# A five-branch decoder layer on one Trainium2 core: gate projections of three branches made earlier and kept in DRAM, and units between the steps of a triangular inverse

## The chip, the cores and the metric

One Trainium2 chip, one of its cores. The metric is the device time of one execution of the whole kernel in microseconds (us), lower is better. Three executions of the kernel before took 3696.6 to 3701.26 us, median 3699.76 us.

## What is computed

One decoder layer over 2048 tokens of width 1024. A normalised input h is projected once by a wide matrix; the columns are shared out among five branches (`mem`, `ret`, `rwkv`, `ssd`, `gla`) and five gates of 1024 columns each. Every branch makes an output o_m of 512 (mem: 256) columns; the gated sum of their up-projections goes through an output matrix. Cut to what matters here:

```
h = rms_norm(x, norm_g)
p = h @ w_in                      # branch inputs, and gates: 5 x 1024 columns
o_m = branch_m(p_m)               # rwkv: a recurrence over time, o_ret, o_gla, o_ssd, o_mem likewise
g = sigmoid(gates).reshape(b, t, 5, d)
merged = sum over m of  g[:, :, m] * (o_m @ w_up_m)
x = x + merged @ w_out
return rms_norm(x, final_norm_g)
```

## The kernel before, in words

Time is cut into four super-chunks of 512 tokens; `run` works through them one after the other, and in each through the branches mem, ret, rwkv, ssd, gla. Data lies as [128 rows of a feature, 512 tokens]. A float32 matrix product is made of three fp32r products of high and low parts (`mm3`), so a **projection** of 128 output columns is 24 matmuls of 128x512 (`proj`, 8 row tiles by 3) and an **up-projection** of 128 columns is 12 (4 row tiles by 3). Weights are split into high and low parts in the first super-chunk (ScalarE `L378`, GpSimd `L379`), stored in DRAM, and from then on loaded from there (`load_w`, two tiles of 512 KB for a projection, one for an up-projection; four buffers `wt`).

For each branch eight gate projections (`gate`: a projection, then ScalarE's tanh into an `s` tile) and eight up-projections (`up`: product, VectorE's scalar_tensor_tensor with the tanh, addition to `merged`) are packed as **units** in a queue `self.fq`, a gate and an up in turn (`inter`). The next branch's code calls `self.fill(n)` at places where its own chain would leave TensorE without work; each call takes n units from the queue. The numbers are in the table `K.FILL`. A scheduler then orders each engine's instructions; the engines run their lists in order. The units' products go to the PSUM tag `acc`, three buffers in turn.

`rwkv` is the branch with the longest chain: `rwkv_prep`, then `rwkv_sys`, which inverts 32 triangular 64x64 matrices at once, then `rwkv_chain` with eight steps. In `rwkv_sys` VectorE runs the **inverse pass**, a serial chain of 31 pairs of multiply and reduce of growing size (`L1195` the reduce) and two transposes (`L1198`, `L1200`); `fill(FILL["sys"][0])` stands behind it, so its units run on TensorE beside it. After the pass, `lower` and `corner` are each four times two sets of eight 32x32 matmuls, with copies by VectorE (`L1215`) and ScalarE between them: the **corner stage**.

At the end of a super-chunk comes the **tail**: the second half of gla finishes (`finish`: a sum by matmul with `ones_r`, a chain of ten VectorE operations, a cast on ScalarE, a subtraction on GpSimd, for each of two heads). In the kernel before the eight gate projections of gla stand there, then eight up-projections of gla, between which the next super-chunk's normalised input `xhi`, `xlo` is made (`xhat_units`; one buffer, so all readers of the old one must be done), then the projections of the next super-chunk. SyncE's queue (SP) issues nearly all DMAs, in order.

```
            us = self.gate_units("gla", o, self.nc.vector if last else None)
            for gate, _ in us:
                gate()
            ...
            for k in range(KT):
                if not last:
                    xu[k]()
                us[k][1]()
```

Of the kernel before, what the change touches and what calls it, by code (L numbers as in the profile page):

```python
# [9 lines left out]
F32 = mybir.dt.float32  # L10
F32R = mybir.dt.float32r
I32 = mybir.dt.int32
AF = mybir.ActivationFunctionType
# [4 lines left out]
P = 128  # L18
T = 512
SEQ = 2048  # L20
D = 1024
KT = D // P
# [53 lines left out]
BR = {"ret": 0, "gla": 1, "ssd": 2, "rwkv": 3, "mem": 4}  # L76
# [68 lines left out]
class K:  # L145
# [131 lines left out]
    def nm(self, s):  # L277
# [2 lines left out]

    NS = 42

    FILL = {"mem": (2, 0, 2, 2, 1, 1, 3, 3), "ret": (1, 3, 0), "late": (0, 0, 0, 0), "sys": (12, 3), "chain":
            (2, 3, 2, 1, 1, 2, 4, 3), "norm": 0, "ssd": (6, 0, 3, 4, 4), "gla": (3, 1, 2, 3, 1), "eng": (0, 1,
            0, 1, 0, 1, 0, 0, 1, 1, 1, 1, 1), "rope": (3, 3)}

# [79 lines left out]
    def pick(self, i):  # L366
        return (self.nc.gpsimd, self.nc.vector)[K.FILL["eng"][i]]

# [184 lines left out]
    def mem(self, sc):  # L553
# [33 lines left out]
        def turn(p, c2, h, e):  # L587
            tp = self.ps("br")
            for j in range(4):
                self.tr(tp[:, j * P:(j + 1) * P], e[:, j * P:(j + 1) * P])  # L590
            t4 = tp.rearrange("p (i m t) -> p i m t", i=2, m=2)
            for m in range(2):
                o4 = pT[p][2 * h + m][:, c2 * 256:(c2 + 1) * 256].rearrange("p (i t) -> p i t", i=2)
                nc.any.tensor_copy(out=o4, in_=t4[:, :, m, :])
# [28 lines left out]
        for i, b in enumerate(blocks):  # L623
            nxt = probs(*blocks[i + 1]) if i < 7 else None
            self.fill(K.FILL["mem"][i])
            turn(*b, e)
            if i == min(K.FILL["rope"][sc > 0], 6):
                self.tables = self.rope_tables(sc)
# [103 lines left out]
    def ret(self, sc):  # L732
# [6 lines left out]
        for p in range(2):  # L739
# [32 lines left out]
            ys = [self.ps("y") for _ in range(2)]  # L772
            self.fill(K.FILL["ret"][0])
            for j in range(2):
                for c in range(4):
                    cs_ = slice(c * P, (c + 1) * P)
                    self.mm(ys[j][:, cs_], V[c][:, (2 * p + j) * P:(2 * p + j + 1) * P], pts[j][:, cs_],
                            start=(c == 0), stop=False)
            self.fill(K.FILL["ret"][1])
            for c in range(4):  # L780
                cs_ = slice(c * P, (c + 1) * P)
                for j in range(2):
                    r = slice(64 * j, 64 * j + 64)
                    self.mm(ys[j][:, cs_], S[c][r, :], qh[r, cs_], start=False, stop=(c == 3))
            res += self.finish_pair(sc, "ret", p, ys, self.cv["one"], K.FILL["ret"][2])
        return res
# [371 lines left out]
    def rwkv_sys(self, AR, KB):  # L1158

        nc = self.nc  # L1160
# [3 lines left out]
        for i in range(4):  # L1164
# [12 lines left out]
            for g in range(4):  # L1177
                r, b = slice(32 * g, 32 * g + 32), g % 2
# [23 lines left out]
        for i in range(4):  # L1202
            for g in range(4):
                r, b = slice(32 * g, 32 * g + 32), g % 2
                (nc.scalar.copy, nc.gpsimd.tensor_copy)[g % 2](
                    Ab[i][r, :, 32 * b:32 * b + 32], xa[r, :, i * 8:i * 8 + 8].rearrange("s c j -> s j c"))
        def lower(i, after=None):
            zp = self.ps("br")
            zs = self.s((P, 8, 32), tag="zs", bufs=2)
            for q in range(2):  # L1210
                r1 = slice(64 * q, 64 * q + 32)
                r2 = slice(64 * q + 32, 64 * q + 64)
                for j in range(8):
                    self.mm(zp[r2, j * 32:j * 32 + 32], Ab[i][r1, j, 32:64], T11[r1, :, i * 8 + j], after=after)
                nc.vector.tensor_copy(zs[r2], zp[r2, 0:256].rearrange("p (j t) -> p j t", t=32))  # L1215
            return zp, zs

        def corner(i, zp, zs):
            for q in range(2):
                r1 = slice(64 * q, 64 * q + 32)  # L1220
                r2 = slice(64 * q + 32, 64 * q + 64)
                for j in range(8):
                    self.mm(zp[r1, 256 + j * 32:256 + j * 32 + 32], zs[r2, j, :], Ab[i][r2, j, 32:64])
                nc.scalar.copy(Ab[i][r1, :, 32:64], zp[r1, 256:512].rearrange("p (j t) -> p j t", t=32))
# [2 lines left out]
        z = lower(0, self.last)  # L1227
        for i in range(4):
            nxt = lower(i + 1) if i < 3 else None
            corner(i, *z)  # L1230
            z = nxt
        return Ab
# [116 lines left out]
        return self.rwkv_fin(sc, BV, sg)  # L1349


    def gate_units(self, key, o, eng=None):
        nc = self.nc
        nk = BRK[key]
        first = self.merged is None
        if first:
            self.merged = [None] * KT
        merged = self.merged
        us = []
        for d in range(KT):  # L1360
            th = []

            def gate(d=d, th=th):
                g = self.proj(f"gate{8 * BR[key] + d}")
                t = self.s()
                self.act(t, g, AF.Tanh, scale=0.5)
                th.append(t)

            def up(d=d, th=th):
                w = self.load_w(("wu_" + key, d), nk)  # L1370
                ps = self.ps("acc")
                self.mm3(ps, w, lambda k: o[k], nk)
                t = th[0]
                if first:
                    m = self.xp.tile([P, T], F32, tag=f"mg{d}", name=self.nm("mg"))
                    merged[d] = m
                    self.stt(m, t, 1.0, ps, ALU.add, ALU.mult)
                else:
                    self.stt(t, t, 1.0, ps, ALU.add, ALU.mult)
                    (eng or self.pick({"ret": 0, "rwkv": 1, "ssd": 2, "gla": 3}[key])).tensor_tensor(  # L1380
                        merged[d], merged[d], t, ALU.add)

            us.append((gate, up))
        return us

    @staticmethod
    def inter(us):

        g, u = [a for a, _ in us], [b for _, b in us]
        out = g[:2]  # L1390
        for i in range(len(us)):
            out.append(u[i])
            out += g[i + 2:i + 3]
        return out
# [130 lines left out]
    def run(self):  # L1525
        for sc in range(self.nsc):
            last = sc + 1 == self.nsc
            self.merged = None
            o = self.mem(sc)
            self.fill(99)  # L1530
            for key, nxt in (("mem", "ret"), ("ret", "rwkv"), ("rwkv", "ssd"), ("ssd", "gla")):
                us = self.gate_units(key, o)
                self.fq += self.inter(us)
                if nxt == "ssd" and not last:
                    rs, self.bg = self.xhat_stats(self.xsrc(sc + 1), T)
                o = getattr(self, nxt)(sc)
                if nxt != "ret":
                    self.fill(99)
            for u in self.bg:
                u()  # L1540
            self.bg = []
            us = self.gate_units("gla", o, self.nc.vector if last else None)
            for gate, _ in us:
                gate()
            if not last:
                self.xh, xu = self.xhat_units(sc + 1, rs[0])
            hl = []
            for k in range(KT):
                if not last:
                    xu[k]()  # L1550
                us[k][1]()
            for k in range(KT):
                hl.append(self.half_split(self.merged[k]))
            self.fq = self.out_units(sc, hl, last)
        self.fill(99)
# [82 lines left out]
```

## Time and profile before

| | |
|---|---|
| median of three executions | 3699.76 us |
| profiled execution | 3696.7 us, of which the span from first to last instruction 3694.9 us |
| TensorE (PE) busy | 3513.3 us, 95% of the span, 20304 matmuls |
| VectorE (DVE) busy | 1978.8 us, 54% |
| ScalarE (ACT), GpSimd (POOL) busy | 984.3 us, 900.1 us |
| mean granted TensorE clock | 0.959 of full |
| DMA | 639.57 MB, mean 173 GB/s |

Busy matmuls are pipelined and their ends are modelled; "idle before" in brackets is the time in which the engine had nothing running, and what ended it. The granted clock (PEclk) is 1.00 at the 2.4 GHz level and 0.50 at the 1.2 GHz level.

### The profile page before, as it was taken

The page shows a single profiled execution, that of the slowest core. Times are in us where ns is not written, and L with a number is a line of the kernel's source. Part 1 is how long each engine was busy: PE and PEld are TensorE (multiplying, and loading weights), DVE is VectorE, ACT ScalarE, POOL GpSimd, SP SyncE. Part 2 cuts the span into 40 slices and gives each one's busy share as a digit, 9 for nine tenths or more (in the row PEclk, how much of TensorE's full clock was granted, in tenths as well). Part 3 has the DMA queues.
Part 4 walks back from the last instruction along what each step waited for, and adds up shares of the span by engine and source line. Part 5 has one row for each costly group of instructions (what it writes and reads, how often), then busy time and mean ns, then how long its engine had stood idle before and what let it go on. Part 6 is the DMA issues. An engine that isn't in the chain of part 4 may idle for free.

```text
span 3694.9 us, 51559 instructions
## 1 busy us (share of the span) xinstructions
PE 3513.3 (95%) x20304; PEld 2805.7 (76%) x20304; DVE 1978.8 (54%) x3189; ACT 984.3 (27%) x1796; POOL 900.1 (24%) x919
## 2 busy tenths in 40 slices
PE   7988898999999999999999999999999998999998
PEld 5766777777777777888877777778887867778887
DVE  6377457635444865653353783663345376464243
ACT  4233224342422311312131322322122132131212
POOL 3556325455311410211101321021100132020110
PEclk9989789999999989999999998999999998999999
DMA  6655435676764533545565552345465554344555
GB/s 216 229 177 199 153 121 203 213 256 220 273 210 153 159 120 112 183 157 168 175 214 176 162 169 91 131 149 187 154 220 181 170 158 130 106 148 151 169 169 193
DMA packets 226530, 639.57 MB, mean 173 GB/s; under 512 B 25184, under 2 KB 46192, under 8 KB 226288
## 3 DMA queue, kind: packets, MB, share of 16 engines
q1 hardware_dynamic: 225856, 635.76, 51.7%
q8 instruction: 160, 2.62, 0.3%
q14 instruction: 82, 0.67, 0.1%
q10 hardware_dynamic: 432, 0.52, 0.0%
HBM read 486.76 MB, written 145.23 MB: 171 GB/s over the span
## 4 chain that ended last, share of the span: by engine, by line
PE 55%; DVE 15%; ACT 2%; issue 1%; DMA 1%; SPq 0%; POOL 0%; DVEq 0%; ACTq 0%
PE acc L305 42%; PE br L305 7%; DVE s L302 7%; PE y L305 4%; DVE s L299 3%; DVE blk L299 2%; DVE blk L1195 1%; PE br L317 1%; ACT s L296 1%; DMA s<-in_xT_dram 1%; DVE s L329 0%; ACT blk L1179 0%; DMA wt<-kw 0%; DVE s L339 0%; DVE s L322 0%
## 5 line engine op out<-in xcount | busy, mean ns | idle before, releaser
L305 PE MATMUL acc<-xhi,wt 128*128 128x512 f32 x5632 | 1834.6, 400 | 46.3 <-DVE s L299 15.8
L305 PEld LDWEIGHTS acc<-xhi,wt 128*128 128x128 f32 x5632 | 1076.2, 192 | 299.1 <-ACT s L296 24.9
L305 PE MATMUL acc<-xlo,wt 128*128 128x512 f32 x2816 | 1126.7, 400 | 2.2 <-DVE xlo L1516 1.5
L305 PEld LDWEIGHTS acc<-xlo,wt 128*128 128x128 f32 x2816 | 539.5, 192 | 117.1 <-issue 4.3
L305 PE MATMUL acc<-s,wt 128*128 128x512 f32 (+1 forms) x2448 | 599.0, 395 | 15.4 <-DVE s L302 7.4
L305 PEld LDWEIGHTS acc<-s,wt 128*128 128x128 f32 x2448 | 454.1, 190 | 115.3 <-ACT wt L378 14.1
L302 DVE SCALAR_TENSOR_TENSOR s<-s,acc 128x512 f32<-128x512 f32 x192 | 131.2, 684 | 632.0 <-PE acc L305 344.5
L379 POOL TENSOR_TENSOR wt<-wr,wt 128x512 fp32r<-128x512 f32 (+1 forms) x256 | 353.2, 1385 | 409.5 <-ACT wt L378 388.5
L302 DVE SCALAR_TENSOR_TENSOR s<-s,s 128x512 f32<-128x512 f32 (+1 forms) x458 | 363.3, 797 | 30.9 <-ACT s L296 18.8
L379 POOL TENSOR_TENSOR s<-s,s 128x512 fp32r<-128x512 f32 x120 | 160.2, 1343 | 888.1 <-ACT s L378 785.2
L296 ACT ACTIVATE s<-acc 128x512 f32<-128x512 f32 x232 | 136.8, 596 | 728.4 <-PE acc L305 728.1
L305 PE MATMUL br<-s,s 64*64 64x64 f32 (+6 forms) x2432 | 238.2, 280 | 6.9 <-DVE s L750 4.2
L1380 POOL TENSOR_TENSOR mg<-mg,s 128x512 f32<-128x512 f32 x64 | 87.8, 1372 | 615.5 <-DVE s L302 615.2
L305 PEld LDWEIGHTS br<-s,s 64*64 64x64 f32 (+3 forms) x2432 | 188.5, 167 | 59.2 <-issue 35.5
L378 ACT CAST wt<-wr 128x512 fp32r<-128x512 f32 (+1 forms) x256 | 155.5, 611 | 266.2 <-PE acc L305 136.9
L296 ACT ACTIVATE s<-s 128x512 f32<-128x512 f32 (+1 forms) x204 | 119.5, 611 | 297.6 <-DVE s L299 123.4
L378 ACT CAST s<-s 128x512 fp32r<-128x512 f32 x182 | 112.8, 620 | 302.0 <-DVE s L302 271.7
L299 DVE TENSOR_TENSOR s<-s 128x512 f32<-128x512 f32 (+1 forms) x167 | 147.4, 886 | 6.1
L305 PE MATMUL y<-s,s 128*64 128x64 f32 (+4 forms) x2112 | 139.0, 255 | 7.3 <-DVE s L299 5.1
L305 PEld LDWEIGHTS y<-s,s 128*64 128x64 f32 (+2 forms) x2112 | 114.9, 153 | 36.4 <-DVE s L1287 9.8
L299 DVE TENSOR_TENSOR s<-s,s 128x512 f32<-128x512 f32 (+2 forms) x154 | 120.6, 808 | 38.2 <-ACT s L296 36.4
L317 PE MATMUL br<-cst,s 128*128 128x128 f32 x484 | 81.8, 293 | 42.9 <-DVE s L302 35.5
(218 smaller groups left out, 3286.1 us busy)
## 6 DMA issues: line engine op xcount, KB each, us to landing
wt<-kw SPq DMA_DIRECT2D x712, 512.0 KB, 3.3
kw<-wt SPq DMA_DIRECT2D x240, 512.0 KB, 3.1
wr<-in_wg_dram SPq DMA_DIRECT2D x176, 256.0 KB, 3.8
s<-in_xT_dram SPq DMA_DIRECT2D x88, 256.0 KB, 4.9
out_dram<-s SPq DMA_DIRECT2D x24, 256.0 KB, 2.6
wt<-kw SPq DMA_DIRECT2D x24, 256.0 KB, 3.0
s<-s SPq DMA_DIRECT2D x64, 64.0 KB, 2.0
bvd<-s SPq DMA_DIRECT2D x16, 256.0 KB, 2.9
```

Source lines behind the costliest of these rows:

```text
L296: self.nc.scalar.activation(out, in_, f, bias=bias, scale=scale, **kw)
L299: self.nc.vector.tensor_tensor(out, a, b, op)
L302: self.nc.vector.scalar_tensor_tensor(out, a, s, b, op0, op1)
L305: i = self.nc.tensor.matmul(out, lhsT=lhsT, rhs=rhs, start=start, stop=stop)
L317: self.nc.tensor.transpose(out, in_, self.c["ident"])
L378: self.nc.scalar.copy(hi, src)
L379: (eng or self.nc.gpsimd).tensor_tensor(lo, src, hi.bitcast(F32), ALU.subtract)
L1195: nc.vector.tensor_reduce(X[:, s_, s_ + 1:], pv, AX.X, ALU.add)
L1380: (eng or self.pick({"ret": 0, "rwkv": 1, "ssd": 2, "gla": 3}[key])).tensor_tensor(merged[d], merged[d], t, ALU.add)
```

## The change

The gates become a method of their own. Those of rwkv, ssd and gla are `far`: their tanh is stored to DRAM (`gth`) and loaded back one up-projection ahead. The eight rwkv gates are made inside rwkv itself, the ssd gates beside the rwkv up-projections in ssd, the gla gates beside the ssd up-projections in gla; the tail keeps only the up-projections of gla. `FILL["sys"]` goes from (12, 3) to (15, 2, 1): 15 units beside the inverse pass, 2 ahead of the corner stage, and 1 ahead of each of the four corners.

```
-    FILL = {... "sys": (12, 3), "chain": ...
+    FILL = {... "sys": (15, 2, 1), "chain": ...
@@ rwkv_sys
         for i in range(4):
             nxt = lower(i + 1) if i < 3 else None
+            self.fill(K.FILL["sys"][2])
             corner(i, *z)
@@ in place of gate_units
+    def gates(self, key, far=False):
+        nc = self.nc
+        th = [None] * KT
+        def gate(d):
+            g = self.proj(f"gate{8 * BR[key] + d}")
+            t = self.s()
+            self.act(t, g, AF.Tanh, scale=0.5)
+            if far:
+                th[d] = self.dp.tile([P, T], F32, name=self.nm("gth"), tag=f"gth_{key}_{d}")
+                nc.sync.dma_start(th[d], t)
+            else:
+                th[d] = t
+        def get(d):
+            if far and d < KT:
+                t = self.s()
+                nc.sync.dma_start(t, th[d])
+                th[d] = t
+        return [lambda d=d: gate(d) for d in range(KT)], th, get
+    def ups(self, key, o, gates, eng=None):
...
+            def up(d=d):
+                if d == 0:
+                    get(0)
+                get(d + 1)
                 w = self.load_w(("wu_" + key, d), nk)
...
@@ run
+            G = {key: self.gates(key, key not in ("mem", "ret")) for key in BR}
             for key, nxt in (("mem", "ret"), ("ret", "rwkv"), ("rwkv", "ssd"), ("ssd", "gla")):
-                us = self.gate_units(key, o)
-                self.fq += self.inter(us)
+                us = self.ups(key, o, G[key])
+                if key in ("mem", "ret"):
+                    self.fq += self.inter(G[key][0], us)
+                else:
+                    self.fq += self.inter(G[nxt][0], us)
+                if nxt == "rwkv":
+                    self.fq += G["rwkv"][0]
...
-            us = self.gate_units("gla", o, self.nc.vector if last else None)
-            for gate, _ in us:
-                gate()
+            us = self.ups("gla", o, G["gla"], self.nc.vector if last else None)
```

**PE at the end of the inverse pass, second super-chunk.** In these names a product of `xhi`, `xlo` is a projection, one of `s` tiles with `wt` an up-projection, `br<-blk` a set of `lower`, `br<-s,zs` a set of `corner`. Before:

```order
L305 MATMUL acc_11096<-s_9815,wt_11094 128x512
L305 MATMUL acc_11096<-s_9816,wt_11094 128x512
L305 MATMUL acc_11096<-s_9815,wt_11094 128x512
L305 MATMUL br_11111<-blk_11028,s_10625 32x32 x8
L305 MATMUL br_11131<-blk_11028,s_10648 32x32 x8
L305 MATMUL br_11169<-blk_11028,s_10671 32x32 x8
L305 MATMUL acc_11363<-xhi_8038,wt_11359 128x512
L305 MATMUL acc_11363<-xlo_8039,wt_11359 128x512
L305 MATMUL acc_11363<-xhi_8038,wt_11359 128x512 x2
L305 MATMUL br_11111<-blk_11028,s_10625 32x32 x8
```

Now, where the up-projection that was the last one is acc_11172:

```order
L305 MATMUL acc_11172<-s_9911,wt_11170 128x512
L305 MATMUL acc_11211<-xhi_8118,wt_11207 128x512
...
L305 MATMUL acc_11240<-s_9911,wt_11238 128x512
L305 MATMUL br_11255<-blk_11189,s_10721 32x32 x8
L305 MATMUL br_11275<-blk_11189,s_10744 32x32 x8
L305 MATMUL acc_11299<-xhi_8118,wt_11295 128x512
...
L305 MATMUL br_11255<-s_10721,zs_11256 32x32 x8
L305 MATMUL br_11344<-blk_11189,s_10767 32x32 x8
L305 MATMUL acc_11366<-s_9626,wt_11364 128x512
```

One projection and one up-projection more stand ahead of the first `lower`, and among the sets of the corner stage lie two projections and two up-projections (acc_11299, 11366, 11423, 11470) where before it was 11 matmuls of one projection (acc_11363). From the corner stage to chain step 1 the order of before holds the rest of that projection (13 matmuls) and one up-projection, the order of now a whole projection and an up-projection.

**PE in the tail, second super-chunk.** Before, behind the last projection of gla itself (acc_14838):

```order
L305 MATMUL acc_14838<-xhi_8038,wt_14836 128x512
L305 MATMUL br_14867<-s_14791,ones_r 128x512
L305 MATMUL br_14867<-s_14792,ones_r 128x512
L305 MATMUL br_14889<-s_14797,ones_r 128x512
L305 MATMUL br_14889<-s_14798,ones_r 128x512
L305 MATMUL acc_14915<-xhi_8038,wt_14911 128x512
L305 MATMUL acc_14915<-xlo_8039,wt_14911 128x512
```

Now:

```order
L305 MATMUL br_15313<-s_15221,ones_r 128x512
L305 MATMUL br_15313<-s_15222,ones_r 128x512
L305 MATMUL acc_15348<-s_14922,wt_15346 128x512
...
L305 MATMUL acc_15348<-s_14944,wt_15346 128x512
L305 MATMUL acc_15372<-s_14922,wt_15370 128x512
...
L305 MATMUL acc_15396<-s_14944,wt_15394 128x512
L305 MATMUL acc_15348<-s_15309,wt_15346 128x512
L305 MATMUL acc_15348<-s_15310,wt_15346 128x512
```

The eight gate projections behind the sums are gone. Three up-projections follow at once, of each the 6 matmuls of the first two heads (18 in all); then the 9 matmuls that read the third head (s_15309, s_15310, the split output of the finish chain), then the 9 of the fourth, then five whole up-projections.

**SP in the tail, second super-chunk**, now (before, the loads of `in_xT` stood alone between the weights):

```order
L434 DMA wt_15418<-kw_8222 128x1024
L507 DMA s_15337<-in_xT_dram 128x512
L1371 DMA s_15342<-gth_14391 128x512
L1371 DMA s_15344<-gth_14424 128x512
L507 DMA s_15363<-in_xT_dram 128x512
L1371 DMA s_15368<-gth_14505 128x512
```

The loads of the stored tanh follow the weights of the fourth up-projection, the first six of them ahead of the weights of the fifth.

## Rows read from the trace of the kernel before

**Rows 1.** The page: busy time, share of the span and count of each engine; TensorE's granted clock in 40 slices of the span, in tenths.
```profile
PE 3513.3 (95%) x20304; PEld 2805.7 (76%) x20304; DVE 1978.8 (54%) x3189; ACT 984.3 (27%) x1796; POOL 900.1 (24%) x919
PEclk9989789999999989999999998999999998999999
```

**Rows 2.** Busy time by stretch (us from the start), second super-chunk: the inverse pass, its end, the corner stage with the first step of the chain; then the gates and the up-projections of the tail; and the middle of the chain. Columns: length, busy time (and instructions) of PE, PEld, DVE, ACT, POOL, granted clock, DMA share, GB/s.
```profile
1290.00:1332.00 42.00, 39.88 (x176) 32.46 (x174) 40.04 (x67) 2.99 (x5) 2.69 (x2) 1.00 0.60 189
1332.00:1339.00 7.00, 0.54 (x9) 0.41 (x9) 6.96 (x6) 1.52 (x3) 2.69 (x4) 0.83 0.74 254
1339.00:1370.00 31.00, 31.00 (x307) 24.26 (x304) 7.11 (x16) 7.95 (x17) 4.84 (x7) 0.50 0.06 19
...
1797.00:1842.00 45.00, 44.83 (x198) 36.79 (x197) 14.86 (x21) 5.70 (x10) 2.70 (x2) 1.00 0.56 187
1842.00:1864.00 22.00, 22.00 (x99) 18.22 (x98) 17.92 (x29) 5.10 (x9) 0.00 (x0) 1.00 0.84 288
...
1400.00:1450.00 50.00, 49.95 (x528) 37.89 (x526) 30.16 (x60) 9.60 (x19) 3.82 (x3) 1.00 0.28 91
```

**Rows 3.** PE in order of time, second super-chunk: two units of the pass, the first `lower`, and the first matmuls of chain steps 1 and 2. Columns: start, us, what, and in brackets the idle time before it and its releaser.
```profile
1323.66 0.50 PE L305 MATMUL acc<-xhi,wt 128*128 128x512 f32 x1 [2.12 <-DVE s L302]
...
1329.27 2.88 PE L305 MATMUL acc<-s,wt 128*128 128x512 f32 x12
1338.62 2.88 PE L305 MATMUL br<-blk,s 32*32 32x32 f32 x48 [6.46 <-DVE blk L1200]
...
1376.55 1.71 PE L305 MATMUL br<-s,s 64*128 64x128 f32 x16
...
1396.30 1.71 PE L305 MATMUL br<-s,s 64*128 64x128 f32 x16
```

**Rows 4.** DVE at the end of the same pass: its last multiply, a unit's scalar_tensor_tensor behind it, the second transpose.
```profile
1331.96 1.80 DVE L299 TENSOR_TENSOR blk<-blk,blk 128x961 f32<-128x961 f32 x1
1333.67 0.67 DVE L302 SCALAR_TENSOR_TENSOR s<-s,acc 128x512 f32<-128x512 f32 x1
...
1337.26 1.20 DVE L1200 STREAM_TRANSPOSE blk<-blk 128x1024 f32<-128x1024 f32 x1
```

**Rows 5.** The same places in other super-chunks: DVE in the first, PE in the first (the first `lower`, chain step 1) and in the third (the first `lower`).
```profile
388.95 3.01 DVE L299 TENSOR_TENSOR blk<-blk,blk 128x961 f32<-128x961 f32 x1
391.89 0.67 DVE L302 SCALAR_TENSOR_TENSOR s<-s,acc 128x512 f32<-128x512 f32 x1
...
396.83 2.88 PE L305 MATMUL br<-blk,s 32*32 32x32 f32 x48 [5.25 <-DVE blk L1200]
...
436.87 1.71 PE L305 MATMUL br<-s,s 64*128 64x128 f32 x16
...
2222.72 2.88 PE L305 MATMUL br<-blk,s 32*32 32x32 f32 x48 [6.47 <-DVE blk L1200]
...
```

**Rows 6.** The tail of the second super-chunk in order of time: the sums of gla's last two heads on PE, the last operation of each head's finish chain (POOL), the eight up-projections and the next super-chunk's first projection (PE), and DVE's first and last operations beside the up-projections (42 of 128x512 between them).
```profile
1796.13 1.07 PE L305 MATMUL br<-s,ones_r 128*128 128x512 f32 x4
...
1805.36 1.42 POOL L379 TENSOR_TENSOR s<-s,s 128x512 fp32r<-128x512 f32 x1 [16.28 <-PE acc L305]
1813.26 1.28 POOL L379 TENSOR_TENSOR s<-s,s 128x512 fp32r<-128x512 f32 x1 [6.48 <-issue]
...
1841.01 21.92 PE L305 MATMUL acc<-s,wt 128*128 128x512 f32 x96
1862.77 0.39 PE L305 MATMUL acc<-xhi,wt 128*128 128x512 f32 x1
...
1844.00 0.69 DVE L302 SCALAR_TENSOR_TENSOR s<-s,acc 128x512 f32<-128x512 f32 x1 [31.53 <-PE acc L305]
...
1867.29 3.69 DVE L302 SCALAR_TENSOR_TENSOR s<-mg,s 128x512 fp32r<-128x512 f32 x6
```

**Rows 7.** What a pause of PE does to the granted clock: two pauses ahead of projections, each with the stretches that follow (columns as in Rows 2).
```profile
380.84 0.75 PE L305 MATMUL acc<-xhi,wt 128*128 128x512 f32 x1 [2.33 <-DVE s L302]
381.00:383.00 2.00, 2.00 (x5) 1.61 (x6) 1.97 (x2) 0.00 (x0) 2.00 (x1) 0.50 0.00 0
383.00:385.00 2.00, 2.00 (x7) 1.55 (x6) 1.93 (x3) 0.00 (x0) 2.00 (x2) 0.68 0.00 0
...
1960.04 0.79 PE L305 MATMUL acc<-xhi,wt 128*128 128x512 f32 x1 [4.62 <-DVE s L299]
1960.00:1965.00 5.00, 4.96 (x12) 3.93 (x13) 1.18 (x2) 0.00 (x0) 1.28 (x1) 0.53 0.82 287
```

**Rows 8.** The tail of the first super-chunk: the sums on PE, the last operation of the finish chain (POOL), the gate projection that waited longest (PE), and the stretch behind it.
```profile
903.89 1.07 PE L305 MATMUL br<-s,ones_r 128*128 128x512 f32 x4
...
926.20 1.27 POOL L379 TENSOR_TENSOR s<-s,s 128x512 fp32r<-128x512 f32 x1 [4.24 <-ACT s L378]
926.67 0.79 PE L305 MATMUL acc<-xhi,wt 128*128 128x512 f32 x1 [5.39 <-ACT s L296]
926.00:931.00 5.00, 4.33 (x11) 3.46 (x12) 0.00 (x0) 2.09 (x5) 2.54 (x2) 0.56 0.17 69
```

**Rows 9.** DMA: loads of weights and of x tiles (KB each, median us from issue to landing); and what the SP queue waited for (us, times, longest).
```profile
wt<-kw SPq DMA_DIRECT2D x712, 512.0 KB, 3.3
s<-in_xT_dram SPq DMA_DIRECT2D x88, 256.0 KB, 4.9
SPq L434 <- PE acc L305: 1938.1, 637, 33.3
```

More of the change, by code (lines that the diff above doesn't have):

```diff
@@ L281 @@
     NS = 42
-    FILL = {"mem": (2, 0, 2, 2, 1, 1, 3, 3), "ret": (1, 3, 0), "late": (0, 0, 0, 0), "sys": (12, 3), "chain":
+    FILL = {"mem": (2, 0, 2, 2, 1, 1, 3, 3), "ret": (1, 3, 0), "late": (0, 0, 0, 0), "sys": (15, 2, 1), "chain":
             (2, 3, 2, 1, 1, 2, 4, 3), "norm": 0, "ssd": (6, 0, 3, 4, 4), "gla": (3, 1, 2, 3, 1), "eng": (0, 1,
@@ L1349, in rwkv @@
         return self.rwkv_fin(sc, BV, sg)
-    def gate_units(self, key, o, eng=None):
+    def gates(self, key, far=False):
         nc = self.nc
+        th = [None] * KT
[15 more added lines that the diff above has]
+    def ups(self, key, o, gates, eng=None):
         nk = BRK[key]
+        _, th, get = gates
         first = self.merged is None
@@ L1360, in gate_units @@
         for d in range(KT):
[L1361 to L1369, printed above, removed]
+            def up(d=d):
+                if d == 0:
+                    get(0)
+                get(d + 1)
                 w = self.load_w(("wu_" + key, d), nk)
@@ L1372, in up @@
                 self.mm3(ps, w, lambda k: o[k], nk)
-                t = th[0]
+                t = th[d]
                 if first:
@@ L1381, in up, with inter @@
                         merged[d], merged[d], t, ALU.add)
-            us.append((gate, up))
+            us.append(up)
         return us
     @staticmethod
-    def inter(us):
-        g, u = [a for a, _ in us], [b for _, b in us]
+    def inter(g, u):
         out = g[:2]
-        for i in range(len(us)):
+        for i in range(len(u)):
             out.append(u[i])
@@ L1550, in run @@
                     xu[k]()
-                us[k][1]()
+                us[k]()
             for k in range(KT):
```

## The prediction, made before the changed kernel ran

> **What bounds the kernel now.** Read the page first: TensorE is busy 95% of the span and no other engine more than 54% [rows 1]. So the end is set by what TensorE does, by its few pauses, and by the clock at which it works; the clock row dips once in each super-chunk [rows 1]. All matmuls before are still there after, so the change can only move pauses and clock. I then cut one super-chunk into stretches [rows 2] and read the dip in order of time [rows 3, 4]. One 128x512 matmul takes (1862.77 - 1841.01)/96 = 0.2267 us at full clock [rows 6]; a projection (24) is 5.44 us, an up-projection (12) 2.72.
>
> The dip is the inverse pass and the corner stage. TensorE has run out of units at 1329.27 + 2.72 = 1331.99 and waits 6.46 us until the second transpose of VectorE lets the first `lower` start at 1338.62 [rows 3, 4]. From there to 1370 the view of stretches gives 31.0 of 31.0 us busy, but at a granted clock of 0.50 [rows 2]: a full row of busy time in which half of the work is done. Chain step 1 begins at 1376.55 [rows 3]. The first and third super-chunks show the same wait, 5.25 and 6.47 us [rows 5]. The chain behind is dense (49.95 of 50 us, clock 1.00), as are the tail's gates (44.83 of 45) [rows 2].
>
> **What changes there, second super-chunk.** The comparison of the orders says: by chain step 1, 36 more matmuls ahead of the first `lower` and 72 - 11 + 36 - 25 = 72 more behind it, 108 in all, 24.5 us. The other 84 of the 192 moved in a super-chunk go into the chain; that is dense at full clock, so they cost there the 19.0 us that they save in the tail. Price of the stretch from 1331.99 on:
> - The added projection needs one of three `acc` buffers. It comes free with the scalar_tensor_tensor that VectorE does behind its last multiply, at 1333.67 + 0.67 = 1334.34 [rows 4]: 2.35 us of wait. Projection and up-projection, 8.16 us, end at 1342.5. The transpose ended at 1338.46 [rows 4], so the wait of 6.46 us is covered.
> - Corner stage: 72 x 0.2267 = 16.3. Its 16 sets of 32x32 matmuls appear in the trace as 16 each (48 for three, 2.88 us, 60 ns each at half clock [rows 3]): 256 x 30 ns = 7.7 at full clock. For the more frequent changes of shape I choose 1.0; bounds 0 and 0.2 for each set, 3.2.
> - Chain step 0: 36 x 0.2267 = 8.16, and its own work, which I take from step 1: 1396.30 - 1376.55 = 19.75 [rows 3] less its 60 large matmuls (13.6) is 6.15.
>
> Sum: 2.35 + 8.16 + 16.3 + 7.7 + 1.0 + 8.16 + 6.15 = 49.8, so step 1 at 1381.8. That is 5.3 us later than now with 24.5 us more done: 19.2 gained. Off this I take 1.0 for the clock: of two pauses of such length one (2.33 us) was followed by 2 us at 0.50 and 2 at 0.68, which is 1.6 lost [rows 7]; the other (2.12, ahead of 1323.66 [rows 3]) stands in a stretch at 1.00 [rows 2]. Gain 18.2; the third and fourth super-chunks are taken alike: 54.6.
>
> First super-chunk: the `acc` buffer is free at 391.89 + 0.67 = 392.56, projection and up-projection end at 400.7. The pass, which ends now at about 396.8, may end up to 3 x 1.2 later, since there GpSimd splits weights for the added units, and a multiply beside such work takes 3.01 against 1.80 [rows 4, 5]; 400.4 is still covered. Step 1 comes at 400.7 + 39.3 = 440.0 against 436.87 [rows 5]: 21.4 gained, less 2.5 that I choose for waits on split weights (bounds 0 and 5): 18.9. All gains: 73.5.
>
> **The clock, as the term that all of this hangs on.** The row shows half clock through a stage that was never idle by the view of stretches [rows 2], so a busy row alone doesn't prove full clock; by the row the added 72 matmuls could run at either level. The Trainium skill (TensorE: Matmul & The Clock Gate, "Why this matters for your kernels") says that TensorE keeps its rate when it is kept busy without long pauses, and loses it by one. By it the pause of 6.46 us caused the dip, and with 2.35 in its place the corner stage would run at full clock; the trace agrees in that the dip begins behind this pause, and leaves open why it lasted. I take full clock, because the pause is gone and because the chain, as mixed in its shapes (528 instructions in 50 us), holds 1.00 [rows 2]. With full clock the sum is the one below, 3677; with half clock it is rival A's, 3740.
>
> **What the tail loses.** With the gates gone only 28 matmuls (6.35 us) can run between the sums of gla's last two heads and GpSimd's last subtraction, since three up-projections have buffers and the other 68 need the fourth head or stand behind it. In the second super-chunk that stretch is 1796.13 + 1.07 = 1797.20 to 1813.26 + 1.28 = 1814.54 [rows 6]: 17.34 us, 11.0 of it idle. The restart: behind a pause of 4.62 us five us went at 0.53 [rows 7], 2.35 lost. So 13.3, and 40 for three super-chunks. In the first, the stretch is 903.89 + 1.07 to 926.20 + 1.27, 22.5 us [rows 8]: 22.5 - 6.35 + 2.4 = 18.6. There the present tail already has a pause of 5.39 and 5 us at 0.56 [rows 8], 7.6 together, which go: 11 lost. All losses: 51.
>
> Behind the restart 68 matmuls take 15.4 us. VectorE has 42 operations there, now from 1844.00 to 1867.29 + 3.69 = 1870.98 [rows 6], 27 us. It would start at about 1815.2 with the first up-projection; the last part of `xlo` is the 31st behind it in the changed order, 31 x 27/42 = 19.9, at 1835.1. TensorE begins the next projection at 1814.5 + 15.4 + 2.35 = 1832.3 and reads that part in its last eighth, 4.8 later. So it fits with 2.0 to spare, and I cost it at 0; if not, rival B.
>
> **The DRAM detour.** 24 stores and 24 loads of 256 KB in each super-chunk are added to SP's queue. I cost them at 0. SP spends 1938 us waiting until TensorE frees a weight buffer [rows 9], so it has time; a weight has three tiles' work (8.2 us) from its buffer's release to its use and takes 3.3, so a store waiting for its tanh may hold it up by 4.9 us. In the tail the first six loads stand ahead of the weights of the fifth up-projection and can go at about 1797, 17 us ahead of use, at 4.9 each [rows 6, 9]; that the stretch at 288 GB/s keeps the DMA engines 84% busy [rows 2] bounds how much can come at once: 11 tiles in 17 us are 170 GB/s. Without that lead: rival C.
>
> **Sum.** 73.5 - 51 = 22.5 less. The profiled execution took 3696.7, its span 3694.9; so 3674. The median of the runs is 3.1 higher, so **3677 us**. Differences under 0.2% (7.4 us) can't be told from none. The likeliest case has its own range from the terms' bounds: 3658 (no wait for the buffer, 2.35 x 4, no clock loss in the tails, 2.35 x 4) to 3692 (the corner stage enters at half clock for 5 us, 2.5 x 4, and 5 of waits on split weights).
>
> **Rivals.**
> - A, slower: the corner stage stays at half clock as long as now, 1338.62 to 1370, 31.4 us. That does 15.7 us less work in each super-chunk, 63 in all: 3740. For it: the stage is at 0.50 with no pause within [rows 2]. Against: the pause ahead of it goes. It decides from 22.5/4 = 5.6 us lost, that is 11.2 us at half clock per super-chunk. Chance 0.10.
> - B: VectorE paces the end of the tail, and the next projection waits for the last `xlo`, 5 us in three super-chunks: 3677 + 15 = 3692. For it: the margin above is 2.0 us. Against: `xhat` needs no up-projection and VectorE can make some ahead. Chance 0.12.
> - C, slower: the loaded tanh come late. Then each of the last five up-projections has 4.9 us of load against 2.72 of work, 2.2 x 5 x 4 = 44: 3721. Against: the place of the loads in SP's order. It decides from 1.1 us each. Chance 0.06.
> - D: the finish chain is faster without gates beside it, or part of the chain's 84 matmuls falls into its remaining gaps (0.05 in 50 us [rows 2], so little): beyond the good bounds, about 3652. Chance 0.06.
>
> **How the numbers follow.** The forecast case has 0.66, of which 0.64 lies below 3692.4. Faster: 0.64 + D 0.06 = 0.70. Same: 0.02 + B 0.12 = 0.14. Slower: A + C = 0.16. The range 3652 to 3700 takes in the forecast case, B and D, 0.84.
>
> **What would show it.** Right: no pause ahead of the first `lower` but one of about 2 us a projection earlier; granted clock 0.9 or more in the corner stage; about 50 us from the last old unit to chain step 1; in the tail about 11 us without matmuls and some 5 us at half clock behind. Wrong: a corner stage at 0.50 (A); a wait for VectorE ahead of the next super-chunk's projection (B) or for a load of `gth` (C); a pause in the tail much other than 11 us, or a chain that grows by other than 19 us.

## The result: slower by 1.1%, and the profile after

The changed kernel took 3738.85 us in the median (3725.73 to 3744.42), the kernel before on the same chip 3698.18: ratio 1.0106, 95% interval 1.0076 to 1.0135, some 40 us slower. The prediction was 3677, faster. The profiled execution of the changed kernel (span 3723.9) is the shortest of its four and 29.0 us longer than that of before; so the trace shows 29 of the 40 us. Its page, first the engines' busy time, then the granted clock in 40 slices:

```profile
PE 3497.1 (94%) x20304; PEld 2780.2 (75%) x20304; DVE 1971.3 (53%) x3189; ACT 984.1 (26%) x1796; POOL 899.2 (24%) x919
PEclk9988999999999999999999999999999999999998
```

Against [rows 1] the dip in the clock row is gone from the last three super-chunks, and busy time fell by 16 us. Yet the span grew: TensorE now stands idle for 226.8 us, before for 181.6. So look for waits. The second super-chunk by stretch, after (columns as in [rows 2]): inverse pass, its end, two parts of the corner stage, then from chain step 1 to a sum in gla that stands in both orders:

```profile
1290.00:1333.00 43.00, 38.58 (x169) 31.28 (x168) 41.55 (x53) 2.96 (x5) 4.40 (x3) 1.00 0.57 183
1333.00:1343.00 10.00, 6.59 (x23) 4.72 (x22) 1.05 (x2) 5.65 (x10) 5.76 (x9) 0.83 0.32 108
1343.00:1357.00 14.00, 14.00 (x134) 11.04 (x134) 2.38 (x5) 0.96 (x2) 1.26 (x1) 0.88 0.33 105
1357.00:1389.00 32.00, 32.00 (x320) 24.88 (x317) 8.93 (x17) 5.07 (x12) 2.72 (x2) 1.00 0.42 135
1389.45:1629.69 240.24, 233.39 (x1698) 186.00 (x1697) 118.18 (x219) 59.16 (x109) 25.95 (x37) 1.00 0.50 159
```

The last stretch in the kernel before:

```profile
1376.55:1590.63 214.08, 212.55 (x1611) 169.88 (x1611) 121.10 (x222) 56.58 (x104) 30.79 (x40) 1.00 0.43 140
```

PE after, in order of time: the last unit that stood there before too, the two added units, sets of the corner stage, chain step 1:

```profile
1324.04 2.88 PE L305 MATMUL acc<-s,wt 128*128 128x512 f32 x12
1329.22 0.50 PE L305 MATMUL acc<-xhi,wt 128*128 128x512 f32 x1 [2.31 <-DVE s L302]
...
1338.41 4.60 PE L305 MATMUL acc<-s,wt 128*128 128x512 f32 x12 [3.41 <-ACT s L296]
1342.94 1.98 PE L305 MATMUL br<-blk,s 32*32 32x32 f32 x32
...
1347.64 1.07 PE L305 MATMUL br<-blk,s 32*32 32x32 f32 x16
...
1356.64 0.69 PE L305 MATMUL br<-s,zs 32*32 32x32 f32 x16
...
1389.45 1.71 PE L305 MATMUL br<-s,s 64*128 64x128 f32 x16
```

ScalarE after, at the same time: eight copies of the inverse, then two tanh in one row:

```profile
1332.44 5.29 ACT L1205 COPY s<-blk 32x256 f32<-32x256 f32 x8 [18.18 <-DVE blk L1198]
1337.76 1.09 ACT L296 ACTIVATE s<-acc 128x512 f32<-128x512 f32 x2
```

Read these two together. The first added unit waits 2.31 us for VectorE, as forecast (2.35). The second waits 3.41 us for a tanh whose projection had ended at 1324: ScalarE was idle for 18 us, but in its order the tanh stands behind eight copies that wait for the transpose. Behind the two pauses the up-projection takes 4.60 us in place of the 2.88 of the one at 1324.04. TensorE's waits after (us, times, longest) have no line for `blk` any more (before: 24.6), but these:

```profile
PE acc L305 <- ACT s L378: 27.4, 8, 4.5
PE acc L305 <- ACT s L296: 20.1, 9, 4.9
PE br L305 <- DMA s<-vtd: 14.4, 15, 1.9
PE acc L305 <- POOL wt L379: 8.6, 3, 6.3
```

The first line is the tail's pauses, which were forecast. The other three stood at 15.0, 1.9 and below 1 us before. `vtd` is a tensor in DRAM of which each of the eight chain steps loads its part; `wt` behind GpSimd's `L379` is a split weight. The longest wait of the last line stands in the first super-chunk, ahead of the first `lower` there, and has the same pattern as the tanh, on GpSimd (GpSimd, then PE):

```profile
396.56 5.13 POOL L1205 COPY s<-blk 32x256 f32<-32x256 f32 x8 [1.94 <-DVE blk L1198]
401.77 3.74 POOL L379 TENSOR_TENSOR wt<-wr,wt 128x512 fp32r<-128x512 f32 x3
403.09 1.22 PE L305 MATMUL acc<-xhi,wt 128*128 128x512 f32 x2 [6.28 <-POOL wt L379]
```

The split of the added projection's weight stands in GpSimd's order behind its own eight copies of the inverse.

The tail after, to be held against [rows 6] (sums, up-projections, next super-chunk's first projection), and the stretch of its pauses:

```profile
1834.90 1.07 PE L305 MATMUL br<-s,ones_r 128*128 128x512 f32 x4
1835.81 4.24 PE L305 MATMUL acc<-s,wt 128*128 128x512 f32 x18
1844.13 0.79 PE L305 MATMUL acc<-s,wt 128*128 128x512 f32 x1 [4.08 <-ACT s L378]
1845.66 3.78 PE L305 MATMUL acc<-s,wt 128*128 128x512 f32 x8 [0.74 <-POOL s L379]
1852.01 0.80 PE L305 MATMUL acc<-s,wt 128*128 128x512 f32 x1 [2.56 <-ACT s L378]
1853.41 17.71 PE L305 MATMUL acc<-s,wt 128*128 128x512 f32 x68 [0.61 <-POOL s L379]
1871.04 0.47 PE L305 MATMUL acc<-xhi,wt 128*128 128x512 f32 x1
```
```profile
1834.90:1860.00 25.10, 17.11 (x53) 12.32 (x52) 20.86 (x31) 3.07 (x5) 2.72 (x2) 0.73 0.55 186
```

| second super-chunk, after minus before, us | predicted | measured |
|---|---|---|
| end of the last old unit to first `lower` | +3.9 | 16.2 - 6.6 = +9.6 |
| first `lower` to chain step 1 | +1.4 | 46.5 - 37.9 = +8.6 |
| chain step 1 to gla | +19.0 | 240.2 - 214.1 = +26.2 |
| tail: sums to next projection | -30.2 | 36.1 - 66.6 = -30.5 |

The column of the forecast leaves out its 1.0 for the clock. The tail is as forecast in sum: 8.0 us of pauses in place of 11.0, and half clock between them. The inverse and the chain are 20.1 us worse than forecast, in three places.

### The profile page after: what moved, and what is told of

Same layout as the page of the kernel before. It is cut to its first block, busy times and chain, and to the rows that moved or that the text cites. A ratio compares the mean times of both kernels' runs of the same rounds, so it can differ in the third digit from the quotient of the medians.

```text
span 3723.9 us, 52005 instructions
## 1 busy us (share of the span) xinstructions
PE 3497.1 (94%) x20304; PEld 2780.2 (75%) x20304; DVE 1971.3 (53%) x3189; ACT 984.1 (26%) x1796; POOL 899.2 (24%) x919
## 4 chain that ended last, share of the span: by engine, by line
PE 66%; DVE 19%; DMA 5%; issue 4%; ACT 4%; POOL 1%; SPq 1%; DVEq 0%; ACTq 0%; POOLq 0%
PE acc L305 52%; PE br L305 8%; DVE s L302 8%; PE y L305 5%; DVE s L299 4%; DVE blk L299 2%; DMA s<-vtd 2%; ACT s L296 2%; DVE blk L1195 1%; PE br L317 1%; DMA s<-in_xT_dram 1%; POOL wt L379 1%; DVE s L329 1%; DMA wt<-kw 1%; ACT blk L1179 0%
## 5 line engine op out<-in xcount | busy, mean ns | idle before, releaser
L305 PE MATMUL acc<-s,wt 128*128 128x512 f32 (+1 forms) x2448 | 624.0, 406 | 61.5 <-ACT s L378 27.4
L305 PEld LDWEIGHTS acc<-s,wt 128*128 128x128 f32 x2448 | 469.9, 197 | 175.2 <-ACT s L378 31.6
L379 POOL TENSOR_TENSOR wt<-wr,wt 128x512 fp32r<-128x512 f32 (+1 forms) x256 | 351.9, 1381 | 401.0 <-ACT wt L378 372.8
L379 POOL TENSOR_TENSOR s<-s,s 128x512 fp32r<-128x512 f32 x120 | 160.2, 1343 | 832.3 <-ACT s L378 750.5
L305 PE MATMUL br<-s,s 64*64 64x64 f32 (+6 forms) x2432 | 219.1, 271 | 26.2 <-DMA s<-vtd 14.4
L305 PEld LDWEIGHTS br<-s,s 64*64 64x64 f32 (+3 forms) x2432 | 175.6, 161 | 74.5 <-issue 46.4
L305 PE MATMUL acc<-wt,xhi 128*128 128x512 f32 x384 | 119.5, 392 | 5.7 <-DVE s L302 3.1
```

Of the source, the lines that this page charges most:

```text
L305: i = self.nc.tensor.matmul(out, lhsT=lhsT, rhs=rhs, start=start, stop=stop)
L379: (eng or self.nc.gpsimd).tensor_tensor(lo, src, hi.bitcast(F32), ALU.subtract)
```

## Experiments

Theory W: three things, each at its place, took back the gain: the tanh behind the copies, sets and changes of shape in the corner stage that cost more than forecast, and late vtd loads in the chain. Each ratio is to the kernel before on the same chip (3700.1 to 3700.6 us), with its 95% interval; the changed kernel itself has 1.0106. "Less" and "more" are against 3739, the changed kernel on that scale (3700 x 1.0106). That base is known to some 11 us only (its interval), and all these differences share it; where it matters, two runs are compared with each other.

| run | median us | ratio, interval |
|---|---|---|
| e1 units as before | 3751.5 | 1.0140, 1.0113 to 1.0166 |
| e2 one unit ahead | 3729.3 | 1.0067, 1.0049 to 1.0086 |
| e3 stores by ScalarE's queue | 3747.4 | 1.0120, 1.0099 to 1.0140 |
| e4 two gates held | 3712.1 | 1.0030, 1.0020 to 1.0039 |
| e5 copies on GpSimd | 3717.0 | 1.0051, 1.0035 to 1.0067 |
| e6 vtd by GpSimd's queue | 3715.1 | 1.0039, 1.0024 to 1.0054 |
| e7 four gates held | 3714.5 | 1.0038, 1.0023 to 1.0053 |
| e8 e5 + e6 + e7 | 3673.9 | 0.9924, 0.9908 to 0.9941 |
| e9 before + e5, e6 | 3700.1 | 1.0002, 0.9992 to 1.0012 |
| e10 e5 + e6 | 3695.6 | 0.9987, 0.9976 to 0.9997 |
| e11 e10 + two gates held | 3680.0 | 0.9951, 0.9935 to 0.9968 |
| e12 e10, none between corners | 3737.2 | 1.0104, 1.0089 to 1.0120 |

**e1**

```
-"sys": (15, 2, 1)
+"sys": (12, 3, 0)
```


> The changed kernel with the old numbers 12, 3 (and 0 between the corners) for the units around the inverse pass; the six units taken out come behind the chain. Theory W (from the two traces: what the new places gained was given back at once, by an up-projection that waits for a tanh, by 32x32 sets that cost 1.0 us each at either clock, and by late vtd loads in the chain): the wait of 6.5 us and the half clock come back, and the time stays within 10 us of the changed kernel, 3727 to 3747. Theory of the prediction (18 us gained in each super-chunk at this place, and lost elsewhere by something not yet seen): 73 us slower, about 3810.

12 us more, with intervals that overlap, and 4.5 above the range that theory W gave. The wait for `blk` is back (20.3 us in 4 places), and so are the dips of the clock. The prediction's gain at this place would have made it 73. So in the kernel as changed the new places of the units are worth about 3 us in each super-chunk, which can't be told from none. Little was lost elsewhere to hide a larger gain: TensorE's waits for vtd are 9.1 us here, 5.3 less than in the changed kernel. Theory W's "1.0 us each at either clock" holds for the sets of `lower` only (rows of 1.09 us before, at 0.50, and of 1.07 after, at 1.00); those of `corner` take 1.05 and 0.69.

**e2**

```
-"sys": (15, 2, 1)
+"sys": (15, 1, 1)
```


> The changed kernel with 15, 1, 1: the up-projection that waited 3.4 us for a tanh no longer stands ahead of the first lower, only the projection does. Theory W: the wait of 3.4 us, and the half clock behind it (1.9 in that up-projection, about 1.4 in the corner stage), go in three super-chunks, 6.7 each, so 20 us less than the changed kernel, about 3717. Rival (the wait only moves to the next user of that buffer): within 5 us of the changed kernel.

10 us less, between the two, with intervals that overlap. The up-projection now stands behind two sets of `lower` and still waits for the same tanh. PE, and a stretch of the corner stage behind it:

```profile
1356.46 1.22 PE L305 MATMUL acc<-s,wt 128*128 128x512 f32 x2 [1.56 <-ACT s L296]
```
```profile
1361.00:1369.00 8.00, 8.00 (x61) 5.89 (x60) 1.10 (x2) 0.72 (x2) 1.27 (x1) 0.50 0.18 66
```

Half of the wait is left, and the clock fell to 0.50 behind it, although large matmuls lie among the sets as before. Moving the waiter is not moving the cause.

**e3**

```
-                nc.sync.dma_start(th[d], t)
+                nc.scalar.dma_start(th[d], t)
```


> The changed kernel with the stores of the tanh issued from ScalarE's queue, right behind the tanh itself, in place of SP's. Theory W: SP no longer waits for ScalarE (76 us in all), the vtd loads of the chain are issued in time, TensorE's waits for them (14.4 us in 15 places) go back to about 2 and those for weights (5 us) to 3: 15 us less than the changed kernel, about 3722. Rival (the added 50 MB themselves cost the time, or nothing does on that side): within 5 us of the changed kernel, with the vtd waits still there.

A miss: no gain, and the vtd waits are there still:

```profile
PE br L305 <- DMA s<-vtd: 19.4, 16, 1.8
```

SP's waits for ScalarE at the stores (76.4 us after the change) are gone from this run, and it is no faster: they cost nothing that can be seen. The vtd loads are late for another reason.

**e4** (`far` is the list of the 24 far gates; rwkv takes `far[:8 - HOLD]`, ssd and gla the next eight each)

```
+    HOLD = 2
+            for gate in far[24 - K.HOLD:]:
+                gate()
             us = self.ups("gla", o, G["gla"], ...)
```


> The changed kernel with every far gate made two places later, so that the last two gate projections of gla stand in the tail between the sums and the up-projections, and two units fewer in rwkv. Theory W: their 10.9 us fill the pause of 11 us, and the restart at half clock (2.4) goes: 13 us less in each of four super-chunks, 52 in all, about 3685. Rival (the finish chain gets slower beside them, or the up-projections wait for something else): less than half of that, above 3711.

27 us less: about half of the 52, and 1 us above the rival's bound of 3711. The trace shows the rival's second condition, up-projections that wait for something else. PE in the tail:

```profile
1852.53 0.80 PE L306 MATMUL acc<-s,wt 128*128 128x512 f32 x1 [3.15 <-ACT s L379]
1853.94 11.01 PE L306 MATMUL acc<-s,wt 128*128 128x512 f32 x38 [0.61 <-POOL s L380]
1866.29 11.16 PE L306 MATMUL acc<-s,wt 128*128 128x512 f32 x48 [1.34 <-DMA wt<-kw]
```

The gates take `acc` buffers, so only 10 matmuls of up-projections ran ahead of GpSimd's last subtraction where 28 did, and the weights of the last four come 1.34 us late: 5.1 us of pauses are left of 8.0.

**e5**

```
-        for i in range(4):
-            for g in range(4):
+        for g, i in [(g, i) for g in (1, 3, 0, 2) for i in range(4)]:
...
-                (nc.scalar.copy, nc.gpsimd.tensor_copy)[g % 2](
+                nc.gpsimd.tensor_copy(
```


> The changed kernel with the eight copies that ScalarE makes behind the first transpose (5.3 us, ahead of two tanh in its order) given to GpSimd, behind the eight that GpSimd makes already. TensorE's order is not touched. Theory W: the tanh come at once, the up-projection ahead of the first lower no longer waits 3.4 us, nor runs at half clock; the first lower comes 5.3 us earlier and the corner stage is 1 to 2 us shorter, in three super-chunks: 20 us less than the changed kernel, about 3720. Rival (the wait of 2.3 us ahead of the projection is enough to bring half clock, or GpSimd's sixteen copies hold up the corners): within 8 us of the changed kernel.

As expected, 22 us less. PE at the place, and the corner stage's first stretch:

```profile
1339.67 0.50 PE L305 MATMUL acc<-xhi,wt 128*128 128x512 f32 x1 [2.29 <-DVE s L302]
...
1345.25 2.88 PE L305 MATMUL acc<-s,wt 128*128 128x512 f32 x12
1348.06 1.98 PE L305 MATMUL br<-blk,s 32*32 32x32 f32 x32
```
```profile
1348.00:1362.00 14.00, 14.00 (x149) 11.03 (x149) 2.80 (x6) 1.32 (x3) 7.05 (x10) 1.00 0.35 116
```

The same order on TensorE, no wait for ScalarE, 2.88 in place of 4.60, and 1.00 in place of 0.88. The pause of 2.29 alone brought no half clock. A comparison that leaves the base out: e10, which has this edit and e6's, is 20 us below e6. In the first super-chunk the edit has a price: GpSimd makes sixteen copies there (9.14 us) ahead of the weight's split, and TensorE's wait for it is 10.28 us in place of 6.28.

**e6**

```
-            nc.sync.dma_start(UV[0:64], self.vtd[...
+            nc.gpsimd.dma_start(UV[0:64], self.vtd[...
```


> The changed kernel with the eight vtd loads of each chain issued from GpSimd's queue in place of SP's, where they stand behind weights that wait for a buffer. Theory W: the waits of TensorE for vtd (14.4 us in 15 places) go to 2 or less: 12 us less than the changed kernel, about 3727. Rival (these loads are late because the DMA engines are full): waits still there, within 5 us of the changed kernel.

24 us less, more than expected:

```profile
PE br L305 <- DMA s<-vtd: 3.3, 3, 1.9
```

With e3 this says: not the stores and not full DMA engines, but the loads' place in SP's order. That weights waiting for buffers ahead of them are what holds them up is argued from SP's in-order queue, not shown by a run of its own. e10, which has this edit and e5's, is 21 us below e5, so the gain stands without the base too. The stretch from chain step 1 to gla got shorter by 5 to 11 us in each of the last three super-chunks; in the second it is now

```profile
1398.28:1631.56 233.28, 229.21 (x1698) 185.33 (x1697) 119.06 (x219) 59.51 (x109) 29.17 (x43) 1.00 0.51 164
```

Of the 7.0 us only 2.8 are idle time; the same 1698 matmuls at the same clock kept TensorE busy 4.2 us less. So the gain is more than the 11 us of waits, and why the busy part shrank stays open.

**e7**: `HOLD = 4`.

> The changed kernel with every far gate made four places later, so that four gate projections of gla (21.8 us) stand in the tail behind the sums. Two of them brought 28 us; they left waits of 5 us, since only 9 matmuls of up-projections ran ahead in place of 28. Theory W: four cover the finish chain (17 us) wholly, nothing of the tail's loss of 12.7 us is left, in four super-chunks: 48 us less than the changed kernel, about 3690. Rival (the tail loses by the weights instead, DMA being full there): 3705 to 3715, no better than with two.

A miss: 25 us less, no better than two. PE in the tail, then VectorE:

```profile
1856.61 12.77 PE L306 MATMUL acc<-s,wt 128*128 128x512 f32 x48 [3.38 <-DVE s L303]
```
```profile
1847.42 0.75 DVE L303 SCALAR_TENSOR_TENSOR s<-s,par,xrs 128x512 f32<-128x512 f32 x1 [12.00 <-DMA s<-in_xT_dram]
```

The finish chain is covered, but VectorE now waits 12.00 us for the first x tile of the next super-chunk, which stands ahead of the up-projections' sums in VectorE's order; their `acc` buffers fill, and TensorE waits for VectorE. That is near the prediction's rival B: VectorE sets the pace at the end of the tail, but through a load, and the one who waits is an up-projection, not the next super-chunk's projection. The time fits the rival of this run, and its cause, late weights, isn't the one seen here. In the second super-chunk the tail itself did gain more than with two: it takes 50.2 us with four projections in it, 41.9 with two, 36.1 with none, so 7.7 and 5.1 us less than the 5.44 us of each projection would make it.

**e8**

> The last three edits together: copies on GpSimd, vtd loads on GpSimd's queue, four gates held for the tail. Theory W: 48 + 20 + 12 = 80 us less than the changed kernel, about 3660, which is 40 under the kernel before. If the parts hide one another: 3680 to 3700.

65 us less, and 26 under the kernel before: the fastest kernel of the study. The parts sum to 22 + 24 + 25 = 71. The 80 of theory W had counted 48 for the held gates.

**e9**

> The kernel before, with two edits that helped the changed one: the copies behind the first transpose all on GpSimd, and the vtd loads on GpSimd's queue. Theory W: in the kernel before no unit waits for a tanh there, and the vtd waits are 1.9 us in all, so nothing is to be had: within 7 us of the kernel before. Rival (these two edits help by themselves, whatever stands around them): 20 to 40 us less, 3660 to 3680.

Even. The two waits are the change's own making, not old ones.

**e10**

> The changed kernel with the same two edits and nothing else. Theory W: the two gains, 21 and 23 us, lie in different places and add up: 3696, within 5 us; so the change without these two waits is about even with the kernel before. Rival (they share a cause, SP's queue): 3710 to 3716.

As expected: 43 us less, against 22 + 24, so the two gains add up, and the change with both edits is 4.6 us under the kernel before, at the limit of what can be told. The two waits are much smaller here and not wholly gone: vtd still 6.6 us in 7 places.

**e11**

> The same with two gates held for the tail in place of the four of the run with all edits. Four left a wait of 3.4 us for VectorE in the tail or 4.2 us for weights; with two in the changed kernel the tail lost 7.3 us. Theory W: 28 us less than the run with the two edits alone, 3668. Rival (the waits of the tail depend on the number held and four is better): 3676 or more.

A miss by 12: 16 us less than e10, where two held gates brought 27 in the changed kernel. The time lies in the rival's range. Whether two or four is better beside the other edits is not settled: the intervals touch.

**e12**

```
-"sys": (15, 2, 1)
+"sys": (15, 2, 0)
```


> The changed kernel with the two edits, and 15, 2, 0: no units between the corners; the four units taken out come behind the chain. No pause stands ahead of the first lower any more, and the corner stage is as thin as in the kernel before. If the pause of 6.5 us brought the half clock, the stage from the first lower to chain step 1 now runs at full clock: 37.9 us by the trace of before, less 11.6 that half clock cost it, about 26.5; the time is then 5 to 12 us less than the run with the two edits alone, since fewer changes of shape are left. If the thin stage itself loses the clock, it takes 33 to 38 us at about 0.5, and the time is 25 to 45 us more. Theory W takes the second: in the second super-chunk of the changed kernel the clock fell to 0.83 within the stage.

Theory W's case: 42 us more than e10. (The 0.83 that it names is the stretch ahead of the stage; within the stage it was 0.88.) What lies ahead of the stage is alike in both: the last pause of TensorE, and in e12 the first `lower` (first row e10, then e12):

```profile
1340.91 0.50 PE L305 MATMUL acc<-xhi,wt 128*128 128x512 f32 x1 [0.75 <-DVE s L302]
1348.59 0.50 PE L305 MATMUL acc<-xhi,wt 128*128 128x512 f32 x1 [0.73 <-DVE s L302]
1356.97 2.89 PE L305 MATMUL br<-blk,s 32*32 32x32 f32 x48
```

The end of the pass and the corner stage by stretch in e12:

```profile
1352.00:1357.00 5.00, 5.00 (x24) 3.87 (x22) 1.42 (x2) 0.60 (x1) 4.90 (x9) 1.00 0.58 202
1357.00:1359.80 2.80, 2.80 (x50) 2.71 (x49) 1.54 (x4) 0.00 (x0) 2.76 (x6) 1.00 0.74 249
1359.80:1362.00 2.20, 2.20 (x23) 1.66 (x21) 0.83 (x1) 0.00 (x0) 2.12 (x4) 1.00 1.01 364
1362.00:1365.00 3.00, 3.00 (x21) 1.90 (x21) 1.88 (x5) 0.00 (x0) 3.00 (x4) 0.54 0.11 45
1365.00:1370.00 5.00, 5.00 (x78) 4.29 (x78) 0.78 (x2) 1.29 (x4) 0.47 (x1) 0.50 0.19 56
1370.00:1388.00 18.00, 18.00 (x161) 14.18 (x160) 3.08 (x6) 2.57 (x7) 0.00 (x0) 0.50 0.08 30
```

and the whole stage with units between, in e10:

```profile
1349.30:1394.10 44.80, 44.80 (x449) 34.91 (x448) 11.32 (x22) 5.98 (x14) 10.66 (x14) 1.00 0.41 137
```

In e12 TensorE is busy from 8 us ahead of the stage on; the stage starts at 1.00, and 5 us later it is at 0.50 and stays there. With two projections and two up-projections in between it keeps 1.00 throughout, and 72 more matmuls cost 44.8 - 37.6 = 7.2 us there. Behind the chain's step 1 the same 72 cost about 18 us in each super-chunk (second: 250.2 against 232.3 from step 1 to gla). The difference, 10 to 11 us in each of four super-chunks, is the 42. That is the working part of the change.

## Why the prediction was wrong, point by point

- **Cover of the first `lower`: right.** The wait for `blk` is gone, and the wait of 2.35 us for the buffer was 2.31.
- **The step that failed first: "Projection and up-projection, 8.16 us, end at 1342.5".** The prediction asked who frees the projection's buffer, and not who frees the up-projection's. That was a tanh in ScalarE's order behind eight copies: 3.41 us, and half clock behind it. Measured: 22 us by e5, 20 by e10 against e6.
- **The corner stage, mis-sized.** The sets were put at 7.7 us "at full clock", from 60 ns at half clock. A `lower` set does not scale: 48 matmuls took 2.88 us at half clock [rows 3], and 48 took 2.89 at 1.00 in e12. A `corner` set does: 1.05 us for 16 at half clock, 0.69 at 1.00. For both kinds and the changes of shape the stage to chain step 1 took 44.8 us at 1.00 in e10, against 49.8 - 2.35 - 8.16 = 39.3: 5.5 in the second super-chunk and 24 in all four.
- **The clock: right in its value, wrong in its cause.** The stage ran at 1.00 from 1357 on, so rival A did not come. But the prediction gave the pause as the first cause, and only beside it that the chain, mixed in its shapes, holds 1.00; the second reason is the one that e12 bears out. In the first it followed the Trainium skill (TensorE: Matmul & The Clock Gate, "Why this matters for your kernels"), by which TensorE kept busy without long pauses keeps its rate. In e12 it was busy without pauses by the profile and fell to 0.50; with large matmuls between the small ones (e10) it kept 1.00. The trace agrees with the rule in e10 and not in e12, and the measurement decides: a stretch that the profile shows as busy may still end at half clock.
- **The chain: "they cost there the 19.0 us that they save in the tail".** It was 26.2 in the second super-chunk, and 9.3, 26.2, 22.0 and 26.7 in the four, 84 against 76. The price of the work itself was not too low: in e10 the four are 12.1, 18.3, 15.2 and 15.8. The vtd loads came later than before, by their place in SP's queue (e6: 24 us). The prediction had costed what the new DMAs do to SP's weights, rightly near 0 (TensorE's waits for `wt` loads ahead of `acc` went from 2.4 to 3.9 us), and not what the new order does to the other loads there.
- **The tail: right.** 13.3 of loss forecast; measured 43.5 - 30.5 = 13.0, where 43.5 is the 192 matmuls at 0.2267. No wait for `xlo` stands behind it.
- **First super-chunk.** Waits on split weights were given 2.5 us, at most 5; one alone took 6.3 (the longest of the POOL line above), since GpSimd's copies stand ahead of the split. The first `lower` came at 410.1, forecast at 400.7.
- **Sum.** 3677 forecast; with the two overlooked waits cut down the change gives 3695.6 (e10), 19 above it, and the two edits' 43 us make the 3739. The corner stage's miss is of the size of these 19, but that is in part luck: by the table below e10 also loses 15.7 more than forecast ahead of the first `lower` and gets 14.7 back in the chains. None of the four rivals was this case, and 0.16 for slower was too little: two units had been given a price without the order of the engine that feeds them.

The whole profiled executions, from the starts of the same instructions in each trace (us against the kernel before; the forecast's terms put in the same places, its clock loss of 1.0 to the fifth row):

| stretch | forecast | changed kernel | e10 |
|---|---|---|---|
| start to the first `lower` | +6.4 | +13.2 | +22.1 |
| first `lower` to chain step 1, four times | +3.4 | +30.4 | +27.7 |
| chain step 1 to gla, four times | +76.0 | +84.2 | +61.3 |
| tail, sums to next projection, four times | -123.0 | -128.9 | -128.9 |
| next projection to the next first `lower`, three times | +14.7 | +27.6 | +16.0 |
| rest | 0 | +2.5 | +2.7 |
| sum | -22.5 | +29.0 | +0.9 |

## What to carry to other kernels

When a unit is put into a gap, price each resource it needs to start: for every buffer, find the instruction that frees it, and look at what stands ahead of that instruction in its own engine's order; an idle engine can still hold a finished result back. Then list every load that the added work is put ahead of on its queue, not the added ones alone. And try large matmuls within a stage of small ones: in e10 against e12 that was worth 42 us.

## What the runs showed of the hardware

- The clock fell to 0.50 within 5 us in a stage that the profile shows as busy throughout, without a pause in the 8 us ahead of it (e12), and held 1.00 in the same stage with 72 more 128x512 matmuls in it (e10). With those matmuls and a pause of 1.56 us among the sets it was at 0.50 behind the pause (e2).
- 48 matmuls of the `lower` kind took 2.88 us at 0.50 [rows 3] and 2.89 us at 1.00 (e12); 16 of the `corner` kind took 1.05 us at 0.50 (kernel before) and 0.69 us at 1.00 (changed kernel).
- A pause of 2.29 us was followed by no loss of clock in e5, as in one of the two cases of the prediction; behind one of 2.10 us in e10 four us (1330 to 1334) went at 0.57, as in the other.
